# In the G stage of a product-key expert layer: the third product of a group moved behind the next compare, U's low parts taken out of the weight helper, expert selection finished four groups earlier

## The chip, the core and the metric

One core of a Trainium2 chip runs the whole program. The metric is the device time of one execution in microseconds (us), the median of several runs. TensorE (PE) multiplies matrices, VectorE (DVE) does elementwise work, ScalarE (ACT) does activations and copies, GpSimd (POOL) here mostly issues gathers, SyncE (SP) issues DMA transfers. Each engine works through its own list of instructions in a fixed order, and waits on semaphores where it needs a result of another.

## What is computed

The reference is one decoder layer on 512 tokens of 1024 features: a pooling mixer and latent attention, an output projection with layer norm, and then a product-key expert layer (PEER), which is where the change lies:

```python
q = (xc @ w_peer_q).reshape(TOK_CHUNK, PEER_HEADS, 2, PEER_HALF)
sc = jnp.einsum('thpd,hpnd->thpn', q, peer_keys)
s1, i1 = lax.top_k(sc[:, :, 0], PEER_TOPK)
s2, i2 = lax.top_k(sc[:, :, 1], PEER_TOPK)
...
s, j = lax.top_k(cand, PEER_TOPK)                 # 16 of 256 pairs, per head
idx = jnp.take_along_axis(cidx, j, axis=-1)       # 8 heads x 16 experts of 16384
gate = jax.nn.softmax(s, axis=-1)
a = jax.nn.gelu(jnp.einsum('thkd,td->thk', peer_u[idx], xc))
return jnp.einsum('thk,thkd->td', gate * a, peer_v[idx])
```

## The kernel before

Tokens lie in four tiles of 128. For the last tile (number 3) the kernel gathers the chosen rows of U and V. For tiles 0 to 2 it computes all 16384 experts densely: gelu(U h) for 128 blocks of 128 experts (a "U step" each), times a gate matrix G that is zero where an expert was not chosen, times V. Products that need float32 precision are made of three matmuls (`mm3`, L193: high by high, L196; high by low, L197; low by high, L198). High is the value rounded on ACT (`split`, L208), low is the rest, subtracted on DVE (`low`, L205).

The **G stage** builds the gate matrix and writes it to DRAM (`Gd`). `g_tiles` (L1061) runs over 3 tiles of 32 groups of four tokens. In iteration q it does, in program order:

- DVE: a compare of the iota row with the two expert indices of group q (`is_equal`, L1072, 1024 columns), which writes one-hot rows 0 and 1 of a buffer `o`; then for group q-1 the products of one-hot row 1 with two bf16 pieces of the gate (L1076, 1024 columns, into rows 2 and 3), and in place with the third piece (L1077, 512 columns). L1077 overwrites what L1076 reads.
- PE: twelve small bf16 matmuls of group q-4 (L1084), four tokens by three pieces. The first two of a token need L1076, the third needs L1077.
- ACT: the copy of group q-5 out of PSUM (L1089); every fourth one is followed by a DMA to `Gd` on SP (L1091).
- DVE: some instructions of the selection of the next tile, `top_second(t + 1)`: a generator whose yields are weights, advanced until their sum reaches `NTP * i` in group i of the tile. With i = 29 (`NQ - 1 - GP`) the rest of it is run, and `g_prep` (L1036) transposes its three results on PE (L1046), copies them on ACT (L1048, L1050) and cuts the gate into pieces on DVE (L1052, L1054).

`beside` (L1106) sets k-steps of U between these: 2.4 of them for an iteration, 8 to a U step, each one `mm3` of 384 columns. A U step (`u_parts`, L797) begins with the gelu of the step before (ACT, L818), then `weights`, which splits the block of the next step: its high part on ACT (L208) and, from here on, its low part on DVE (L205), at once. So ACT waits for PE to end a U step, L208 comes behind that, and L205 behind L208.

Ahead of the G stage the selection of tile 3 and that of tile 0 run side by side on DVE (`both`, L1118), with k-steps of U beside them. Behind it comes the **V stage**, which reads G back and multiplies by V. No planner orders anything: the program order of each engine is that in which the Python code emits it. Buffers come from a pool `F` of 17.

Of the kernel before, what the change touches and what calls it, by code (L numbers as in the profile page):

```python
# [10 lines left out]
F32R = mybir.dt.float32r  # L11
# [3 lines left out]
AF = mybir.ActivationFunctionType  # L15
# [5 lines left out]
P = 128  # L21
# [25 lines left out]
DT = 3  # L47
# [12 lines left out]
N_S2 = 33  # L60
SCF = 15
NPRE = 2
NTP = 0.36
GP = 2
NPRE2 = 8

# [83 lines left out]
def trace(ctx: ExitStack, tc: tile.TileContext, A, out):  # L150
# [28 lines left out]
    def wide(dt=F32, shape=(P, D)):  # L179
        return T("F", shape, dt)  # L180
# [12 lines left out]
    def mm3(o, pairs, first=True, last=True):  # L193
        n = len(pairs)
        for i, (lh, ll, rh, rl) in enumerate(pairs):
            pe.matmul(o, lh, rh, start=first and i == 0, stop=False)  # L196
            pe.matmul(o, lh, rl, start=False, stop=False)  # L197
            pe.matmul(o, ll, rh, start=False, stop=last and i == n - 1)  # L198
# [8 lines left out]
    def split(hi, lo, src, eng=None):  # L207
        act.activation(hi, src, AF.Copy)  # L208
        low(lo, src, hi, eng)


    jobs, live, ueng = [], {}, [pool]
    done = {"load": 0, "split": 0}

    def job(src, shape=(P, KD, P), eng=None, dst=None):
# [11 lines left out]
    def split_to(i):  # L227
        while done["split"] < min(i, len(jobs)):
            n = done["split"]
            load_to(n + 1)  # L230
            _, shape, eng, dst = jobs[n]
            w = live.pop(n)
            if dst is None:
                live[n] = wide(F32R, shape), wide(F32R, shape)
                split(*live[n], w, ueng[n % len(ueng)] if eng == "u" else eng)
            else:
                dst(w)
            done["split"] += 1

    def weights(i, ahead=3):  # L240
        split_to(i + 1)
        load_to(i + 1 + ahead)
        split_to(i + 2)
        return live.pop(i)
# [357 lines left out]
    for m in range(2):  # L602
        wh, wl = weights(juk[m])
        for h in range(3):
            p = bank()
# [191 lines left out]
    def u_parts():  # L797

        i = nu[0]
        if i >= NK or i - max(used[0], NBF) > N_BACK - 2:  # L800
            return
        nu[0] += 1
        while gelus:
            gelus.pop(0)()
        wh, wl = weights(ju[i])
        p = a_bank()[:, :ND]
        for k in range(KD):
            mm3(p, [(wh[:, k], wl[:, k], h2h[k][:, :ND], h2l[k][:, :ND])], first=k == 0, last=k == KD - 1)
            yield

        def gelu():
            if i >= NBF:
                back[i] = T("B", [P, ND])
            else:
                if i % 2 == 0:
                    bf[0] = wide()
                back[i] = bf[0][:, i % 2 * ND:(i % 2 + 1) * ND]
            act.activation(back[i], p, AF.Gelu)  # L818
        gelus.append(gelu)
# [241 lines left out]
    def g_tiles():  # L1061

        PB, L = TB // 4, LL
        oo, pp, parts, stg = {}, {}, {0: g_prep(0)}, None
        rows = lambda x, n: x.rearrange("p a j (i d) -> p (a j) i d", d=2) if n else x
        iota8 = iotab.rearrange("p (i d) -> p i d", d=2).unsqueeze(1).to_broadcast([P, 8, P // 2, 2])
        for q in range(DT * NQ + L + 1):
            t, i = divmod(q, NQ)
            if t < DT:

                o = oo[q] = wide(BF, (P, 4, 4, P))
                dve.tensor_tensor(rows(o[:, :2], 8), iota8, pairs(parts[t][0][:, i], 8), op=ALU.is_equal)  # L1072
            if 1 <= q <= DT * NQ:
                o, g = oo[q - 1], parts[(q - 1) // NQ][1][:, (q - 1) % NQ]
                one = o[:, 1:2].rearrange("p a j i -> p a (j i)").to_broadcast([P, 2, 4 * P])
                dve.tensor_mul(rows(o[:, 2:], 8), one, pairs(g[:, 1:], 8))  # L1076
                dve.tensor_mul(rows(o[:, 1:2], 4), rows(o[:, 1:2], 4), pairs(g[:, :1], 4))  # L1077
            if L <= q < DT * NQ + L:
                o = oo.pop(q - L)
                uid[0] += 1  # L1080
                p = pp[q - L] = psg.tile([P, 4, P], F32, name=f"gp_{uid[0]}", tag="gp", bufs=4)
                for j in range(4):
                    for n in (2, 3, 1):
                        pe.matmul(p[:, j], o[:, 0, j], o[:, n, j], start=n == 2, stop=n == 1)  # L1084
            if q > L:
                r = q - L - 1
                if r % PB == 0:
                    stg = T("G", [P, NK, TB])
                act.activation(stg[:, :, r % PB * 4:r % PB * 4 + 4], pp.pop(r).rearrange("p t i -> p i t"), AF.Copy)  # L1089
                if r % PB == PB - 1:  # L1090
                    sync.dma_start(Gd[:, r // PB], stg)  # L1091
            if t + 1 < DT:
                if i == 0:
                    nxt, spent = top_second(t + 1), 0.0
                while spent < NTP * i:
                    spent += next(nxt, 99.0)
                if i == NQ - 1 - GP:
                    for _ in nxt:
                        pass
                    parts[t + 1] = g_prep(t + 1)  # L1100
            yield KD * R_G[min(t, DT - 1)]

# [204 lines left out]
```

## Time and profile before

| | |
|---|---|
| runs | 1615.81, 1612.07, 1616.0 us; median 1615.81 |
| profiled execution | 1614.81 us, of which the traced span is 1613.1 us |
| mean granted TensorE clock | 0.975 |
| busy in the span | PE 1505.9 us (93%), DVE 1257.4 (78%), ACT 590.5 (37%), POOL 405.3 (25%) |
| G stage | 458.4 to 687.2 us of the span: tile 0 to 537.8, tile 1 to 623.4, tile 2 to the end |

A busy share is an average over stages with different limits, and PE's hides the G stage, where DVE is busier than PE. Times inside the span count from its start. In a timeline the first number is an instruction's start, the second its duration, and what stands in brackets is the idle time of its engine before it and what ended it. Instructions of one engine overlap a little: the distance between two starts is what one costs in a full queue, and it can be shorter than the duration.

### The profile page before, as it was taken

Reading aid. Unit: us, or ns where it says so; the run is one execution under the profiler, and the core shown is the slowest. Engines: PE = TensorE matmul, PEld = TensorE weight load, DVE = VectorE, ACT = ScalarE, POOL = GpSimd, SP = SyncE. Lnnn points to the kernel's source line nnn. Section 1 sums busy time; section 2 is a strip of 40 time slices with the busy share of each in tenths; the row PEclk is TensorE's granted clock in tenths of the full one; section 3 lists DMA queues with packets and bytes.
Section 4 is the critical chain, followed back from the end, with each engine's and each line's share of the span. In section 5 each row is a group of like instructions: output and inputs, shape, how many; then the busy total and the mean of one; then the engine's idle time right before and its main releaser. Section 6 shows DMA issues by size and latency. Waiting matters only on the chain.

```text
span 1613.1 us, 22579 instructions
## 1 busy us (share of the span) xinstructions
PE 1505.9 (93%) x8217; PEld 1294.1 (80%) x8217; DVE 1257.4 (78%) x2717; ACT 590.5 (37%) x909; POOL 405.3 (25%) x315
## 2 busy tenths in 40 slices
PE   5899999699888898969999999999999999999996
PEld 4665678578877777849999888898989888888984
DVE  5666556789999898947686877697788788778797
ACT  3353534223334443423342433343333333333342
POOL 0000101623100000013333343443333233333323
PEclk9999999899999998979999999999999999999998
DMA  8655103542234444689888899889889889888781
GB/s 327 216 183 201 67 26 124 188 128 76 99 106 171 144 180 147 220 265 329 303 318 301 306 320 323 303 315 334 314 286 343 288 315 335 303 317 318 277 302 74
DMA packets 147295, 382.70 MB, mean 237 GB/s; under 512 B 11312, under 2 KB 62544, under 8 KB 144112
## 3 DMA queue, kind: packets, MB, share of 16 engines
q1 hardware_dynamic: 109328, 243.56, 43.7%
q0 software_dynamic: 37856, 137.70, 24.0%
q8 instruction: 64, 1.05, 0.3%
q14 instruction: 47, 0.39, 0.1%
HBM read 351.86 MB, written 29.36 MB: 236 GB/s over the span
## 4 chain that ended last, share of the span: by engine, by line
PE 66%; DVE 23%; issue 3%; DMA 3%; ACT 2%; POOL 2%; SPq 0%; POOLq 0%; DVEq 0%; ACTq 0%
PE acc L197 10%; PE acc L198 10%; PE acc L196 9%; PE a L198 9%; PE a L196 9%; PE a L197 9%; DVE F L205 3%; DVE F L1076 3%; DVE F L1072 3%; PE ps L198 2%; PE ps L197 2%; PE ps L196 2%; DVE F L1077 2%; PE ps L662 1%; PE gp L1084 1%
## 5 line engine op out<-in xcount | busy, mean ns | idle before, releaser
L205 DVE TENSOR_TENSOR F<-F,F 128x1024 fp32r<-128x1024 f32 (+2 forms) x274 | 334.9, 1223 | 90.9 <-ACT F L208 63.6
L196 PE MATMUL a<-H,F 128*128 128x384 f32 (+1 forms) x1040 | 360.8, 347 | 3.9 <-ACT F L208 3.9
L198 PE MATMUL a<-H,F 128*128 128x384 f32 (+1 forms) x1040 | 353.9, 340 | 7.3 <-DVE F L205 5.2
L197 PE MATMUL a<-H,F 128*128 128x384 f32 (+1 forms) x1040 | 352.3, 339 | 0.0
L1137 POOL DMA_INDIRECT F<-in_u,cidx x128 | 159.2, 1243 | 553.3 <-PE acc L198 496.1
L196 PE MATMUL acc<-F,W 128*128 128x512 f32 x696 | 271.5, 390 | 15.3 <-ACT W L1203 15.3
L197 PE MATMUL acc<-F,W 128*128 128x512 f32 x696 | 273.1, 392 | 0.1
L198 PE MATMUL acc<-F,W 128*128 128x512 f32 x696 | 273.0, 392 | 0.0
L1137 POOL DMA_INDIRECT F<-in_v,cidx x128 | 147.9, 1155 | 273.4 <-DVE F L205 171.8
L198 PEld LDWEIGHTS a<-H,F 128*128 128x128 f32 x1040 | 197.4, 190 | 10.4 <-DVE F L205 6.9
L196 PEld LDWEIGHTS a<-H,F 128*128 128x128 f32 x1040 | 198.1, 190 | 8.3 <-ACT F L208 4.2
L197 PEld LDWEIGHTS a<-H,F 128*128 128x128 f32 x1040 | 197.9, 190 | 4.1
L1146 DVE SCALAR_TENSOR_TENSOR F<-F,F 128x1024 f32<-128x1024 f32 x128 | 153.3, 1220 | 59.4 <-DMA F<-in_u,cidx 59.3
L1159 DVE SCALAR_TENSOR_TENSOR Y<-F,a,Y 128x1024 f32<-128x1024 f32 x127 | 163.0, 1283 | 45.8 <-DMA F<-in_v,cidx 43.3
L208 ACT ACTIVATE F<-F 128x1024 fp32r<-128x1024 f32 (+2 forms) x164 | 169.6, 1036 | 54.4 <-DVE Y L1159 12.6
L1201 ACT ACTIVATE F<-F 128x1024 fp32r<-128x1024 f32 x128 | 134.9, 1054 | 144.3 <-DVE F L1146 72.0
L196 PEld LDWEIGHTS acc<-F,W 128*128 128x128 f32 x696 | 131.1, 188 | 40.8 <-ACT W L1203 15.5
L198 PEld LDWEIGHTS acc<-F,W 128*128 128x128 f32 x696 | 131.0, 188 | 27.6 <-DVE W L205 0.2
L197 PEld LDWEIGHTS acc<-F,W 128*128 128x128 f32 x696 | 131.0, 188 | 26.3 <-DVE F L205 0.6
L818 ACT ACTIVATE B<-a 128x384 f32<-128x384 f32 x122 | 59.3, 486 | 209.3 <-PE a L198 197.5
L1203 ACT ACTIVATE W<-B 128x384 fp32r<-128x384 f32 x110 | 57.8, 525 | 212.2 <-PE acc L197 114.0
L1084 PE MATMUL gp<-F 128*128 128x128 bf16 x1152 | 87.4, 221 | 13.3 <-DVE F L1076 6.0
(283 smaller groups left out, 1986.3 us busy)
## 6 DMA issues: line engine op xcount, KB each, us to landing
F<-in_ut SPq DMA_DIRECT2D x128, 512.0 KB
F<-in_v SPq DMA_DIRECT2D x128, 512.0 KB
F<-in_wada SPq DMA_DIRECT2D x48, 512.0 KB
Gd<-G SPq DMA_DIRECT2D x24, 1024.0 KB
G<-Gd SPq DMA_DIRECT2D x15, 1536.0 KB
F<-in_wpq SPq DMA_DIRECT2D x16, 512.0 KB
F<-in_wout SPq DMA_DIRECT2D x8, 512.0 KB
F<-in_win SPq DMA_DIRECT2D x8, 448.0 KB
```

What stands on the lines that cost most here:

```text
L196: pe.matmul(o, lh, rh, start=first and i == 0, stop=False)
L197: pe.matmul(o, lh, rl, start=False, stop=False)
L198: pe.matmul(o, ll, rh, start=False, stop=last and i == n - 1)
L205: dve.tensor_sub(lo, src, f(hi))
L208: act.activation(hi, src, AF.Copy)
L818: act.activation(back[i], p, AF.Gelu)
L1084: pe.matmul(p[:, j], o[:, 0, j], o[:, n, j], start=n == 2, stop=n == 1)
L1137: pool.indirect_dma_start(out=g, out_offset=None, in_=table, in_offset=bass.IndirectOffsetOnAxis(ap=cidx[:, k:k + 1], axis=0))
L1146: dve.scalar_tensor_tensor(g, g, 1.0, h2r[DT], op0=ALU.mult, op1=ALU.mult, accum_out=aT[:, k:k + 1])
L1159: dve.scalar_tensor_tensor(y3, g, aT[:, k:k + 1], y3, op0=ALU.mult, op1=ALU.add)
L1201: act.activation(Vhl[j][0], v, AF.Copy)
L1203: act.activation(W[j][0], w, AF.Copy)
```

## The change

Three edits. In `g_tiles` the product with two pieces now comes first in an iteration, then the compare of the next group, then the product in place. U's low parts, where they belong to DVE, are put on a list; the list is emptied behind the third k-step of the running U step, or at the start of the next. The selection is paced at 0.42 instead of 0.36, and its rest is run at i = 25, while `g_prep` stays at i = 29.

```diff
-NTP = 0.36
+NTP = 0.42
...
-    jobs, live, ueng = [], {}, [pool]
+    jobs, live, ueng, lows = [], {}, [pool], []
...
-                live[n] = wide(F32R, shape), wide(F32R, shape)
-                split(*live[n], w, ueng[n % len(ueng)] if eng == "u" else eng)
+                hi, lo = live[n] = wide(F32R, shape), wide(F32R, shape)
+                if eng == "u" and ueng[0] is dve:
+                    act.activation(hi, w, AF.Copy)
+                    lows.append((lo, w, hi))
+                else:
+                    split(hi, lo, w, ueng[n % len(ueng)] if eng == "u" else eng)
...
+    def low_now():
+        while lows:
+            low(*lows.pop(0))
+
     def weights(i, ahead=3):
+        low_now()
         split_to(i + 1)
...
             mm3(p, [(wh[:, k], wl[:, k], h2h[k][:, :ND], h2l[k][:, :ND])], first=k == 0, last=k == KD - 1)
+            if k == 2:
+                low_now()
             yield
...
             t, i = divmod(q, NQ)
+            if 1 <= q <= DT * NQ:
+                o1, g = oo[q - 1], parts[(q - 1) // NQ][1][:, (q - 1) % NQ]
+                one = o1[:, 1:2].rearrange("p a j i -> p a (j i)").to_broadcast([P, 2, 4 * P])
+                dve.tensor_mul(rows(o1[:, 2:], 8), one, pairs(g[:, 1:], 8))
             if t < DT:
 
                 o = oo[q] = wide(BF, (P, 4, 4, P))
                 dve.tensor_tensor(rows(o[:, :2], 8), iota8, pairs(parts[t][0][:, i], 8), op=ALU.is_equal)
             if 1 <= q <= DT * NQ:
-                o, g = oo[q - 1], parts[(q - 1) // NQ][1][:, (q - 1) % NQ]
-                one = o[:, 1:2].rearrange("p a j i -> p a (j i)").to_broadcast([P, 2, 4 * P])
-                dve.tensor_mul(rows(o[:, 2:], 8), one, pairs(g[:, 1:], 8))
-                dve.tensor_mul(rows(o[:, 1:2], 4), rows(o[:, 1:2], 4), pairs(g[:, :1], 4))
+                dve.tensor_mul(rows(o1[:, 1:2], 4), rows(o1[:, 1:2], 4), pairs(g[:, :1], 4))
...
-                if i == NQ - 1 - GP:
+                if i == NQ - 1 - GP - L:
                     for _ in nxt:
                         pass
+                if i == NQ - 1 - GP:
                     parts[t + 1] = g_prep(t + 1)
```

The order of PE, ACT, POOL and SP is what it was, instruction for instruction; only DVE's list is reordered, from 422 us of the span to the end of the G stage. In the changed program the lines have moved: the compare is L1087, the product with two pieces L1083, the product in place L1089, the selection's first line L961 (before: L950), its last L1038 (L1027), the gate's copies L1063 and L1065 (L1052 and L1054).

First place: DVE in tile 2, where no selection runs. The names F_989, F_996, F_998 are the one-hot buffers of three groups in a row, F_994 is a low part of U. Before:

```order
L205 TENSOR_TENSOR F_994_6151<-F_966_5952,F_993_6150 128x1024
L1072 TENSOR_TENSOR F_996_6161<-iotab_3649,sm2_955_5879 128x1024
L1076 TENSOR_TENSOR F_989_6128<-F_989_6128,gp3_957_5881 128x1024
L1077 TENSOR_TENSOR F_989_6128<-F_989_6128,gp3_957_5881 128x512
L1072 TENSOR_TENSOR F_998_6188<-iotab_3649,sm2_955_5879 128x1024
L1076 TENSOR_TENSOR F_996_6161<-F_996_6161,gp3_957_5881 128x1024
L1077 TENSOR_TENSOR F_996_6161<-F_996_6161,gp3_957_5881 128x512
```

And of the change, the same place:

```order
L1083 TENSOR_TENSOR F_989_6129<-F_989_6129,gp3_957_5880 128x1024
L1087 TENSOR_TENSOR F_996_6161<-iotab_3649,sm2_955_5878 128x1024
L1089 TENSOR_TENSOR F_989_6129<-F_989_6129,gp3_957_5880 128x512
L205 TENSOR_TENSOR F_994_6151<-F_966_5952,F_993_6150 128x1024
L1083 TENSOR_TENSOR F_996_6161<-F_996_6161,gp3_957_5880 128x1024
L1087 TENSOR_TENSOR F_998_6189<-iotab_3649,sm2_955_5878 128x1024
L1089 TENSOR_TENSOR F_996_6161<-F_996_6161,gp3_957_5880 128x512
```

Between the two products of one buffer there now stands the compare of the next, and the low part comes one group later.

Second place: DVE at the end of tile 0, where the selection of tile 1 ends. The names sm_811 and sm_812 (after: sm_797 and sm_798) are its results, sm_814 is the transposed gate. Before:

```order
L1072 TENSOR_TENSOR F_808_4868<-iotab_3649,sm2_685_4036 128x1024
L1076 TENSOR_TENSOR F_806_4842<-F_806_4842,gp3_687_4038 128x1024
L1077 TENSOR_TENSOR F_806_4842<-F_806_4842,gp3_687_4038 128x512
L1020 TENSOR_TENSOR F_756_4453<-F_756_4453,bt_728_4265 128x2x128
L1027 TENSOR_TENSOR sm_811_4888<-F_756_4453 128x128
L1027 TENSOR_TENSOR sm_812_4889<-F_756_4453 128x128
L1052 CAST gp3_815_4894<-sm_814_4893 128x32x8
```

And of the change:

```order
L1038 TENSOR_TENSOR sm_797_4778<-F_746_4395 128x128
L1038 TENSOR_TENSOR sm_798_4779<-F_746_4395 128x128
L1083 TENSOR_TENSOR F_794_4759<-F_794_4759,gp3_687_4038 128x1024
L1087 TENSOR_TENSOR F_799_4789<-iotab_3649,sm2_685_4036 128x1024
L1089 TENSOR_TENSOR F_794_4759<-F_794_4759,gp3_687_4038 128x512
L1083 TENSOR_TENSOR F_799_4789<-F_799_4789,gp3_687_4038 128x1024
L1087 TENSOR_TENSOR F_806_4824<-iotab_3649,sm2_685_4036 128x1024
L1089 TENSOR_TENSOR F_799_4789<-F_799_4789,gp3_687_4038 128x512
L205 TENSOR_TENSOR F_804_4817<-F_776_4628,F_803_4816 128x1024
L1083 TENSOR_TENSOR F_806_4824<-F_806_4824,gp3_687_4038 128x1024
L1087 TENSOR_TENSOR F_808_4849<-iotab_3649,sm2_685_4036 128x1024
```

The two results are made four groups ahead of the gate's first copy (L1063, five rows after the last one shown); before, they stood right in front of it.

Third place: DVE in the second group of tile 1, where the next selection begins. The name sm_833 is what ACT takes the exponential of, F_841 is a low part of U. Before:

```order
L950 TENSOR_TENSOR sm_833_5022<-F_455_2222 128x128
L954 CAST sm_834_5025<-F_455_2222 128x128
L956 TENSOR_SCALAR sm_835_5026<-sm_834_5025 128x128
L205 TENSOR_TENSOR F_841_5039<-F_800_4807,F_840_5038 128x1024
L1072 TENSOR_TENSOR F_843_5046<-iotab_3649,sm2_813_4892 128x1024
```

And of the change:

```order
L961 TENSOR_TENSOR sm_833_5022<-F_455_2222 128x128
L965 CAST sm_834_5025<-F_455_2222 128x128
L967 TENSOR_SCALAR sm_835_5026<-sm_834_5025 128x128
L1083 TENSOR_TENSOR F_830_5004<-F_830_5004,gp3_815_4894 128x1024
L1087 TENSOR_TENSOR F_843_5046<-iotab_3649,sm2_813_4892 128x1024
L1089 TENSOR_TENSOR F_830_5004<-F_830_5004,gp3_815_4894 128x512
L969 TENSOR_SCALAR sm_835_5026<-sm_835_5026 128x128
L971 TENSOR_SCALAR sm_837_5028<-sm_834_5025 128x128
L205 TENSOR_TENSOR F_841_5039<-F_802_4814,F_840_5038 128x1024
```

One whole group and two small instructions now stand between the selection's first three and the low part.

## Rows read from the trace of the kernel before

**Rows 1.** The page: busy time by engine, and shares of the chain that ended last.

```profile
PE 1505.9 (93%) x8217; PEld 1294.1 (80%) x8217; DVE 1257.4 (78%) x2717; ACT 590.5 (37%) x909; POOL 405.3 (25%) x315
...
PE 66%; DVE 23%; issue 3%; DMA 3%; ACT 2%; POOL 2%; SPq 0%; POOLq 0%; DVEq 0%; ACTq 0%
```

**Rows 2.** Windows, one for each tile: length, busy times, granted clock, DMA share, GB/s.

```profile
458.40:537.80 79.40, 66.97 (x571) 58.10 (x570) 76.04 (x153) 32.83 (x53) 0.00 (x0) 0.96 0.40 142
537.80:623.40 85.60, 72.93 (x633) 63.60 (x630) 77.08 (x154) 36.47 (x59) 0.00 (x0) 0.94 0.45 158
623.40:687.20 63.80, 61.74 (x616) 56.09 (x615) 62.41 (x107) 30.09 (x50) 0.00 (x0) 1.00 0.61 215
```

**Rows 3.** Groups by line, DVE, 458.4 to 687.2: busy, mean ns, idle before.

```profile
L1077 DVE TENSOR_TENSOR F<-F,gp 128x512 bf16<-128x512 bf16 x96 | 40.8, 425 | 3.3
L205 DVE TENSOR_TENSOR F<-F,F 128x1024 fp32r<-128x1024 f32 x28 | 34.3, 1225 | 9.0 <-ACT F L208 9.0
```

**Rows 4.** Timeline of DVE in tile 2: start, duration, instruction, idle before.

```profile
647.06 0.68 DVE L1072 TENSOR_TENSOR F<-iotab,sm 128x1024 bf16<-128x1024 bf16 x1
647.66 0.69 DVE L1076 TENSOR_TENSOR F<-F,gp 128x1024 bf16<-128x1024 bf16 x1
648.38 0.43 DVE L1077 TENSOR_TENSOR F<-F,gp 128x512 bf16<-128x512 bf16 x1
648.72 1.22 DVE L205 TENSOR_TENSOR F<-F,F 128x1024 fp32r<-128x1024 f32 x1
```

**Rows 5.** Timeline of DVE ahead of the G stage, two selections side by side.

```profile
443.04 1.28 DVE L1012 TENSOR_TENSOR F<-bt,sm 128x1024 bf16<-128x1024 bf16 x2
444.25 1.28 DVE L1014 TENSOR_TENSOR F<-F,sm 128x1024 bf16<-128x1024 bf16 x2
...
449.06 1.22 DVE L205 TENSOR_TENSOR F<-F,F 128x1024 fp32r<-128x1024 f32 x1
450.20 0.75 DVE L1018 TENSOR_TENSOR F<-F 128x512 bf16<-128x512 bf16 x2
```

**Rows 6.** Timeline of DVE, its idle times at the ends of tiles 0 and 1.

```profile
534.97 1.23 DVE L205 TENSOR_TENSOR F<-F,F 128x1024 fp32r<-128x1024 f32 x1 [1.83 <-ACT F L208]
...
541.11 0.28 DVE L950 TENSOR_TENSOR sm<-F 128x128 f32<-128x128 f32 x1
...
544.52 1.23 DVE L205 TENSOR_TENSOR F<-F,F 128x1024 fp32r<-128x1024 f32 x1 [2.73 <-ACT F L208]
...
622.26 1.23 DVE L205 TENSOR_TENSOR F<-F,F 128x1024 fp32r<-128x1024 f32 x1 [4.22 <-ACT F L208]
```

**Rows 7.** Timeline of PE at the transposes of tile 0's end.

```profile
530.02 0.69 PE L1046 MATMUL tr<-cst,sm 128*128 128x128 f32 x2 [6.90 <-DVE sm L1027]
```

**Rows 8.** Timeline of ACT at the start of tile 1.

```profile
541.43 0.31 ACT L952 ACTIVATE sm<-sm 128x128 f32<-128x128 f32 x1 [1.17 <-DVE sm L950]
```

**Rows 9.** Timeline of PE in tile 2: groups 59, 89, and 90 with 91.

```profile
619.32 0.84 PE L1084 MATMUL gp<-F 128*128 128x128 bf16 x12
...
679.18 0.84 PE L1084 MATMUL gp<-F 128*128 128x128 bf16 x12
...
680.45 1.51 PE L1084 MATMUL gp<-F 128*128 128x128 bf16 x24
```

**Rows 10.** Timeline of PE: three waits ahead of the G stage, one matmul more.

```profile
417.32 0.44 PE L198 MATMUL a<-H,F 128*128 128x384 f32 x1 [2.07 <-POOL F L203]
417.60 0.34 PE L196 MATMUL a<-H,F 128*128 128x384 f32 x1
...
425.33 0.69 PE L196 MATMUL a<-H,F 128*128 128x384 f32 x1 [3.90 <-ACT F L208]
...
450.33 0.69 PE L198 MATMUL a<-H,F 128*128 128x384 f32 x1 [4.92 <-DVE F L205]
```

**Rows 11.** Windows behind the wait of 3.90: columns as in rows 2.

```profile
425.30:430.60 5.30, 5.02 (x14) 4.51 (x15) 5.29 (x21) 1.30 (x2) 0.00 (x0) 0.50 0.36 148
```

**Rows 12.** Timeline of PE: the first matmul of the V stage.

```profile
703.23 0.80 PE L196 MATMUL acc<-F,W 128*128 128x512 f32 x1 [15.30 <-ACT W L1203]
```

## The prediction

> **What bounds the kernel now.** I read the page first: PE is busy 93% of the span and has 66% of the chain that ended last, DVE 23% [rows 1]. That is a mean over stages. The change touches one stage, so I asked for windows, one for each tile of the G stage [rows 2]. The reader is to compare DVE's busy time with the length: 76.0 of 79.4 us in tile 0, 77.1 of 85.6 in tile 1, 62.4 of 63.8 in tile 2, while PE has 67.0 and 72.9 in the first two. So the stage of 228.8 us is set by DVE, and DVE's time there is of two kinds.
>
> First what a group costs in DVE's full queue. Read the starts, not the durations [rows 4]: compare to first product 0.60 us, first product to product in place 0.72, from there to the next instruction 0.34; together 1.66. The compare of 0.68 is overtaken by 0.08, while the product in place starts only 0.03 after the end of the one whose input it overwrites. These 0.03 are the 3.3 us of idle time in front of 96 such products [rows 3]. A low part of U costs 1.14 from start to start (449.06 to 450.20 [rows 5]), and there are 28 [rows 3].
>
> Second its idle time: 9.0 us, all in front of U's low parts, all until ACT has the high part [rows 3]. Three of them make 8.8 [rows 6]. The first comes about so: PE has reached the transposes of the selection, which DVE has not yet finished, and stands for 6.90 us [rows 7]; what follows on PE, the end of a U step, is late, so its gelu on ACT is late, so the high part behind it, so DVE's low part: 1.83 us. The second, 2.73, is in part of another kind: ACT waits in its order for the selection's first instruction (541.11), takes the exponential at 541.43 [rows 8], and only then reaches the gelu and the high part.
>
> **The change, part by part.**
>
> *The product in place behind the next compare.* Nothing is added, nothing removed. The product in place now stands two behind the one that it has to wait for, with a compare between. I take 0.60 for each of the two large ones and 0.34 for the small one: 1.54 instead of 1.66, 0.12 a group. Is a wait on an instruction two places back free? The trace has such pairs: ahead of the G stage two selections run side by side, each L1014 needs the L1012 two places before it, and two of these 1024-column instructions take 444.25 - 443.04 = 1.21, that is 0.60 each [rows 5]. The first compare and its product now stand next to each other, and the last group has no compare behind it, so 94 groups gain: 94 x 0.12 = 11.3 us. The bounds are 0 (every instruction pays for its predecessor's end however they stand) and 11.3; I take the upper, as the pairs are the same kind of instruction.
>
> Here a rule of the Trainium skill speaks against it: VectorE: DVE Perf Modes, section "The DRAIN you can't avoid", says that the next operation does not start until the pipe of the one before is empty, and that chaining without semaphores does not avoid it. By that rule the new order would save nothing. The row disagrees for independent instructions (0.60 between starts, 0.68 of duration), and agrees only for the product in place; the measured starts decide.
>
> *The selection four groups earlier.* The transposes stand where they stood on PE, but their inputs are now made in group 25, and PE's matmuls ahead of them (group 25's) already need a product that DVE makes after that. So the waits of 6.90 go, and with them the lateness of gelu and high part: 1.83 and 4.22 of DVE's idle time, and the 0.2 left over. What is late next? In tile 1's second group ACT still waits for the selection's first instruction. From 541.11 to the low part's start the chain takes 3.41 us [rows 6], of which DVE could use 0.7 before. In the new order there stand the selection's three, one group (1.54) and two small ones between, some 2.4 us; about 1.0 of the 2.73 stays. The denser pacing costs a little: four more selection instructions stand directly behind the one that they wait for, at about 0.1 each: 0.4 us.
>
> *U's low parts later.* They move one group back in DVE's order. Within DVE the order of independent work costs nothing; the cover is that the high part is then surely there. Who waits for it? PE needs the low part at the third matmul of the next U step. PE runs up to three groups ahead of DVE's list; the low part used to be emitted 3.3 groups ahead of its use, now some 2.3, so PE will stand there up to one group (1.7 us) longer in tiles 0 and 1. PE has room: its 32 groups need 32 x 1.995 = 63.8 us at the rate of tile 2 (30 groups from 619.32 to 679.18 [rows 9]), and DVE will need some 74. So this wait replaces waits that PE had group by group. Ahead of the G stage it is not free: PE stands 4.92 us for a low part [rows 10], which now comes behind four half-size selection instructions more (2 x 0.67 from 450.20, taken twice [rows 5]): 1.34 later, less 0.6 which DVE gains there by filling earlier idle time. The G stage starts 0.7 later. Bounds: 0 to 1.4.
>
> *Tile 2, where PE becomes the slower one.* DVE would need 32 x 1.54 + 8 low parts x 1.14 = 58.4, 1.82 a group; PE needs 1.995 as long as U goes on. U ends at group 90 for want of buffers, and groups then take 0.7 [rows 9]. At the start of tile 2 PE stands near group 62: 28 x 1.995 + 1.3 + 5 x 0.7 + 0.7 = 61.4 us to the end of the last group, against 64.5 before (623.4 to 703.23 - 15.30 = 687.9 [rows 2, 12]). Gain 3.1, where DVE alone would give 4.
>
> *The sum.* Tiles 0 and 1: 62 x 0.12 = 7.4, and 8.8 - 1.0 = 7.8 of idle time, less 0.4: 14.8. Tile 2: 3.1. Start: -0.7. Together 17.2 us. Behind the last group everything is as before: the way through DRAM to the first V matmul, 15.30 us in which PE idles [rows 12], and a V stage whose lists are unchanged (in it a U step is emitted as a whole, so the deferred low part has nothing to pass on DVE). The profiled execution took 1614.8 us, span 1613.1 and 1.7 around it: 1614.8 - 17.2 = 1597.6. It lies 1.0 below the median of the runs shown and within them. I forecast 1597.5.
>
> **The rivals.**
>
> *A: the new order of the products saves nothing.* By the rule above. Then only the idle time goes, in tiles 0 and 1, and tile 2 stays DVE's: 7.8 + 0.2 - 0.4 - 0.7 = 6.9, 1608. For it: only that the product in place itself never was measured with something in between. Against it: the pairs [rows 5].
>
> *B: PE or buffers take part of it.* PE's list is 63.8 us a tile and a few transposes; if its waits for low parts don't fall into its free time, tiles 0 and 1 gain half: 1603 to 1606. For it: DVE's and PE's rates in tile 2 lie within a tenth. Against: ten us of room in each of the first two tiles.
>
> *C: slower.* One mechanism: PE's wait for the low part, at the start of each U step of tiles 0 and 1, becomes long enough for the clock to fall. After the waits of 3.90 and 4.92 it did: granted 0.50 (the 1.2 GHz level) for 5.3 us behind the first of them [rows 10, 11]; half of that, 2.6 us, is lost each time. A U step is 3.33 groups: 6.6 of PE work and 2.6 make 9.2, more than DVE's 7.7; 20 steps of it are 184 us for two tiles that took 165. With 3.1 back from tile 2 and 0.7 lost ahead: 1631. It decides if the waits come near those two in length. Against it: I expect under two, and after a wait of 2.07 PE went on at full speed, 0.34 for the next matmul [rows 10].
>
> *D: no change*, because the waits at the transposes turn up elsewhere, as waits of DVE for buffers that PE frees (each compare needs a buffer that PE read five groups before): 1612 to 1618. Against it: PE runs ahead.
>
> **How the numbers follow.** Forecast 0.72 (its own range 1594 to 1601), A 0.07, B 0.12, C 0.04, D 0.05. Differences under 0.3%, 4.8 us, can't be told from none. Forecast, A and B lie beyond it: faster 0.91; D: same 0.05; C: slower 0.04. The range is 1592 to 1607: it takes in B and most of A, and below leaves 2 us for the runs' own spread and for a late start of the G stage that doesn't happen.
>
> **What would show it.** The G stage should last about 212 us instead of 228.8. In its timeline the compare, the product in place and the first product should start 0.60, 0.34 and 0.60 apart, with no idle time in front of the product in place. DVE's idle time until ACT's high parts should be 1 to 2 us instead of 9.0. PE should have no wait for L1038 at the transposes, the granted clock should be 1.00 in tiles 0 and 1, and new waits of PE for DVE's low parts should appear, each under two us. It would be wrong if DVE is under 95% busy in tiles 0 and 1, if PE has waits of over three us there, or if the V stage changes its length.

## The result, and the profile after

The changed kernel takes 1594.41 us (median of four runs, 1592.38 to 1597.79); the kernel before 1615.9 beside it. The ratio is 0.987, 95% interval 0.9847 to 0.9893. The forecast was 1597.5, with a range of 1592 to 1607. A second timing, below, gave 0.9872.

The line numbers have moved: the compare L1072 is now L1087, the product of two pieces L1076 is L1083, the product in place L1077 is L1089, the gate matmuls L1084 are L1096, U's high part L208 is L236 (L205 stays), and the transposes L1046 are L1057.

From the page of the kernel after: busy times, and shares of the chain that ended last [rows 1]. Next to nothing moves here, although 17.2 us of span are gone: the shares are means over 1600 us.

```profile
PE 1504.0 (94%) x8217; PEld 1294.2 (81%) x8217; DVE 1248.0 (78%) x2717; ACT 591.4 (37%) x909; POOL 408.7 (26%) x315
...
PE 67%; DVE 23%; DMA 4%; issue 2%; ACT 2%; POOL 2%; SPq 0%; DVEq 0%; POOLq 0%; ACTq 0%
```

Windows of the kernel after, one for each tile, with the columns of [rows 2]:

```profile
461.00:535.70 74.70, 67.83 (x603) 60.43 (x602) 74.15 (x153) 34.69 (x55) 0.00 (x0) 0.98 0.46 165
535.70:610.50 74.80, 66.62 (x615) 58.49 (x613) 73.37 (x153) 34.30 (x58) 0.00 (x0) 1.00 0.48 174
610.50:670.60 60.10, 59.93 (x603) 55.08 (x602) 60.01 (x107) 30.05 (x50) 0.00 (x0) 1.00 0.59 210
```

Behind the length stand the busy times of PE, of PEld (TensorE's weight loads) and of DVE. DVE now fills 74.15 of 74.70, 73.37 of 74.80 and 60.01 of 60.10 us: the stage is DVE's list and next to nothing else. The granted clock, 0.96 and 0.94 in the first two tiles before, is 0.98 and 1.00.

Groups by line, DVE, over the G stage after (busy, mean ns, idle before), to be read against [rows 3]:

```profile
L1089 DVE TENSOR_TENSOR F<-F,gp 128x512 bf16<-128x512 bf16 x96 | 39.7, 413 | 0.0
L205 DVE TENSOR_TENSOR F<-F,F 128x1024 fp32r<-128x1024 f32 x28 | 34.3, 1223 | 0.9 <-ACT F L236 0.9
```

Both idle times went: 3.3 to 0.0 in front of the product in place, 9.0 to 0.9 in front of the low parts. Timeline of DVE after, in tile 1 and tile 2 (start, duration, instruction, idle before), against [rows 4, 6]:

```profile
541.64 1.23 DVE L205 TENSOR_TENSOR F<-F,F 128x1024 fp32r<-128x1024 f32 x1 [0.92 <-ACT F L236]
...
647.53 0.68 DVE L1083 TENSOR_TENSOR F<-F,gp 128x1024 bf16<-128x1024 bf16 x1
648.13 0.67 DVE L1087 TENSOR_TENSOR F<-iotab,sm 128x1024 bf16<-128x1024 bf16 x1
648.73 0.41 DVE L1089 TENSOR_TENSOR F<-F,gp 128x512 bf16<-128x512 bf16 x1
649.07 1.21 DVE L205 TENSOR_TENSOR F<-F,F 128x1024 fp32r<-128x1024 f32 x1
```

The starts lie 0.60, 0.60 and 0.34 apart, where before it was 0.60, 0.72 and 0.34. PE's waits in the stage after (line, releaser: us in total, times, longest us):

```profile
PE a L198 <- DVE F L205: 12.6, 12, 2.3
PE gp L1096 <- DVE F L1089: 1.9, 6, 0.5
PE tr L1057 <- ACT sm L1059: 0.5, 2, 0.3
```

The waits of 6.9 us at the transposes [rows 7] are gone; in their place PE waits twelve times for a low part, the longest 2.3. Timeline of PE after: the wait ahead of the stage, the longest waits for a low part in tile 0 and in tile 1, and the first matmul of the V stage, against [rows 10, 12]:

```profile
453.08 0.69 PE L198 MATMUL a<-H,F 128*128 128x384 f32 x1 [5.23 <-DVE F L205]
...
489.91 0.44 PE L198 MATMUL a<-H,F 128*128 128x384 f32 x1 [2.34 <-DVE F L205]
490.19 0.84 PE L1096 MATMUL gp<-F 128*128 128x128 bf16 x12
...
493.48 1.44 PE L1096 MATMUL gp<-F 128*128 128x128 bf16 x12
...
560.27 0.45 PE L198 MATMUL a<-H,F 128*128 128x384 f32 x1 [2.23 <-DVE F L205]
560.56 0.84 PE L1096 MATMUL gp<-F 128*128 128x128 bf16 x12
...
685.54 0.80 PE L196 MATMUL acc<-F,W 128*128 128x512 f32 x1 [14.23 <-ACT W L1216]
```

Behind the wait of 2.23 PE goes on at full speed (0.84 for twelve gate matmuls, as in [rows 9]); behind the one of 5.23 a matmul takes 0.69. Behind the wait of 2.34 twelve gate matmuls take 0.84 at first and 1.44 three microseconds later, and a window of the kernel after shows why, with the columns of [rows 2]:

```profile
491.30:494.70 3.40, 3.40 (x20) 3.09 (x19) 3.40 (x8) 0.36 (x1) 0.00 (x0) 0.50 0.02 5
```

The granted clock is 0.50 here, the 1.2 GHz level; this one stretch makes the 0.98 of tile 0. DVE is busy all through it (3.40 of 3.40 us), so it costs the stage no idle time of DVE.

### The profile page after: what moved, and what is told of

The parts are those of the page before. It is cut to its first block, busy times and chain, and to the rows that moved or that the text cites. A ratio compares the mean times of both kernels' runs of the same rounds, so it can differ in the third digit from the quotient of the medians.

```text
span 1595.9 us, 22580 instructions
## 1 busy us (share of the span) xinstructions
PE 1504.0 (94%) x8217; PEld 1294.2 (81%) x8217; DVE 1248.0 (78%) x2717; ACT 591.4 (37%) x909; POOL 408.7 (26%) x315
## 4 chain that ended last, share of the span: by engine, by line
PE 67%; DVE 23%; DMA 4%; issue 2%; ACT 2%; POOL 2%; SPq 0%; DVEq 0%; POOLq 0%; ACTq 0%
PE acc L197 10%; PE acc L198 10%; PE acc L196 10%; PE a L198 9%; PE a L196 9%; PE a L197 9%; DVE F L1083 3%; DVE F L205 3%; DVE F L1087 3%; PE ps L198 2%; PE ps L197 2%; PE ps L196 2%; DVE F L1089 2%; DMA F<-in_v 1%; PE ps L671 1%
## 5 line engine op out<-in xcount | busy, mean ns | idle before, releaser
L205 DVE TENSOR_TENSOR F<-F,F 128x1024 fp32r<-128x1024 f32 (+2 forms) x274 | 334.4, 1221 | 89.6 <-ACT F L236 31.7
L1214 ACT ACTIVATE F<-F 128x1024 fp32r<-128x1024 f32 x128 | 134.9, 1054 | 146.1 <-DMA F<-in_v 67.1
L236 ACT ACTIVATE F<-F 128x1024 fp32r<-128x1024 f32 x120 | 126.5, 1054 | 30.5 <-DVE Y L1172 14.2
L198 PE MATMUL ps<-H,F 128*128 128x512 f32 x176 | 74.3, 422 | 11.5 <-POOL F L203 6.2
```

The costliest lines, as they stand in the source:

```text
L205: dve.tensor_sub(lo, src, f(hi))
L236: act.activation(hi, w, AF.Copy)
L1214: act.activation(Vhl[j][0], v, AF.Copy)
```

## The experiments

All tables here come from the traces of single executions. A tile lasts from its first compare to the next tile's, the stage from the first compare to the end of the last gate matmul; "idle" is DVE's idle time inside the stage, counting gaps above 0.06 us. "Ratio" is the measured time over that of the kernel before. Three theories were put to the test. M is the prediction's: DVE's list sets the stage, so the new order of the products and the idle time in front of the low parts are two gains that add up. R is the rule that the new order saves nothing. P says that PE's two waits of 6.9 us at the transposes, with the lower clock behind them, are the time, so that the earlier selection alone brings nearly all of it.

| kernel | ratio, 95% | tile 0 | tile 1 | tile 2 | stage | idle |
|---|---|---|---|---|---|---|
| before | | 79.39 | 85.63 | 64.52 | 229.54 | 8.97 |
| products alone | 0.9958 [0.9944, 0.9972] | 76.38 | 82.22 | 62.60 | 221.21 | 12.06 |
| low parts alone | 0.9970 [0.9958, 0.9982] | 77.86 | 80.10 | 65.97 | 223.93 | 3.09 |
| selection alone | 0.9962 [0.9949, 0.9975] | 77.87 | 81.77 | 64.25 | 223.89 | 2.73 |
| products, selection | 0.9898 [0.9883, 0.9912] | 74.64 | 77.77 | 60.08 | 212.49 | 3.05 |
| products, low parts | 0.9898 [0.9884, 0.9912] | 74.76 | 76.32 | 64.78 | 215.85 | 6.46 |
| low parts, selection | 0.9960 [0.9944, 0.9976] | 77.82 | 78.61 | 65.34 | 221.77 | 0.80 |
| all three | 0.9870 [0.9847, 0.9893] | 74.72 | 74.77 | 60.79 | 210.28 | 0.92 |
| low parts later still | 0.9927 [0.9914, 0.9941] | 79.72 | 76.22 | 63.35 | 219.29 | 7.94 |
| every other low part on POOL | 0.9985 [0.9977, 0.9994] | 81.28 | 78.78 | 66.65 | 226.71 | 9.41 |

**The new order of the products alone.** The kernel before with this edit and no other:

```diff
+            if 1 <= q <= DT * NQ:
+                ...
+                dve.tensor_mul(rows(o1[:, 2:], 8), one, pairs(g[:, 1:], 8))
             if t < DT:
                 ...
             if 1 <= q <= DT * NQ:
-                ...
-                dve.tensor_mul(rows(o[:, 2:], 8), one, pairs(g[:, 1:], 8))
-                dve.tensor_mul(rows(o[:, 1:2], 4), rows(o[:, 1:2], 4), pairs(g[:, :1], 4))
+                dve.tensor_mul(rows(o1[:, 1:2], 4), rows(o1[:, 1:2], 4), pairs(g[:, :1], 4))
```

> The kernel before with the first edit alone: product in place behind the next compare. Theory M (DVE sets tiles 0 and 1, PE's backlog sets tile 2): 94 groups x 0.12 us leave DVE's list, of which the backlog that PE has after the transposes of tile 1 takes a little back: 9 to 11 us faster, 1605 to 1607 where before is 1616. The idle time of DVE in front of U's low parts stays at 8 to 10 us. Rival R (an instruction pays for its predecessor's end however they stand): 0, and the first product and the compare start 0.68 or more apart. Rival P (PE is the bound, its waits are what counts): under 3 us.

It took 1608.95 us against 1615.0. R and P fall, but M was too high, and with another reason: the stage lost 8.3 us, not the full 94 x 0.12 = 11.3, and what takes the rest back is not PE's backlog but idle time of DVE, which M had expected to stay at 8 to 10 us and which is 12.06. The idle time in front of the low parts tells why; timeline of DVE in this kernel:

```profile
532.77 1.23 DVE L205 TENSOR_TENSOR F<-F,F 128x1024 fp32r<-128x1024 f32 x1 [2.08 <-ACT F L208]
...
541.94 1.23 DVE L205 TENSOR_TENSOR F<-F,F 128x1024 fp32r<-128x1024 f32 x1 [2.73 <-ACT F L208]
...
616.53 1.23 DVE L205 TENSOR_TENSOR F<-F,F 128x1024 fp32r<-128x1024 f32 x1 [4.76 <-ACT F L208]
622.93 1.23 DVE L205 TENSOR_TENSOR F<-F,F 128x1024 fp32r<-128x1024 f32 x1 [0.56 <-ACT F L208]
```

Before it was 1.83, 2.73 and 4.22 [rows 6], and 0.19 behind them. DVE reaches the low part sooner, ACT's high part is no sooner there, and in tile 2 five waits of 0.41 to 0.56 appear that were not there. Idle time grows by 3.1; 11.3 - 3.1 = 8.2.

**The low parts alone.**

```diff
-                split(*live[n], w, ueng[n % len(ueng)] if eng == "u" else eng)
+                if eng == "u" and ueng[0] is dve:
+                    act.activation(hi, w, AF.Copy)
+                    lows.append((lo, w, hi))
...
+            if k == 2:
+                low_now()
```

> The kernel before with the second edit alone: U's low parts one group later. M: the low part gives the high part 1.7 us more, so of DVE's waits of 1.83 and 2.73 some 3.4 us go; the 4.22 at the end of tile 1 count for nothing, because PE has a backlog there; 0.3 to 0.7 is lost at the start of the G stage: 2 to 4 us faster, 1612 to 1614. PE waits 13.8 us at the transposes as before. P: 0, or slower by the new waits of PE for low parts (some 12 us in all in the changed kernel): 1616 to 1628.

1611.33 against 1615.0, just beyond the expected 1612 to 1614. The stage is 5.6 shorter, which is more than was expected, and the idle time 5.9: the low part behind the third k-step alone takes most of the waits for ACT away, the 4.22 at the end of tile 1 among them, which M had counted for nothing. Of the 3.09 that are left 1.2 are waits for ACT, the rest are waits of compares for buffers that PE frees. Tile 2 grows by 1.4. In this trace the V stage is 2.3 us longer than before, so its span shows only 2.6 of the 5.6.

**The selection alone.**

```diff
-NTP = 0.36
+NTP = 0.42
...
-                if i == NQ - 1 - GP:
+                if i == NQ - 1 - GP - L:
                     for _ in nxt:
                         pass
+                if i == NQ - 1 - GP:
                     parts[t + 1] = g_prep(t + 1)
```

> The kernel before with the third edit alone: selection done four groups ahead of the transposes. M: PE's 13.8 us of waiting go, but only the DVE idle time that they cause counts, 1.83 + 4.22, less 0.4 for the denser pacing: 5 to 6 us faster, 1610 to 1611; the wait of 2.73 behind the exponential stays. P: all of PE's 13.8 us and its slow clock behind them come back: 14 us or more faster, 1602 or less.

1609.58 against 1615.0, as M said; P's 14 us fall. PE's waits at the transposes are gone here (none above 0.3), but only 5.7 of the stage go with them. One idle time of DVE is left in the trace of this kernel, and it is the second of [rows 6], at its old size:

```profile
545.26 1.23 DVE L205 TENSOR_TENSOR F<-F,F 128x1024 fp32r<-128x1024 f32 x1 [2.73 <-ACT F L208]
```

**Products and selection, the low parts as before.** The changed kernel with

```diff
-                if eng == "u" and ueng[0] is dve:
-                    act.activation(hi, w, AF.Copy)
-                    lows.append((lo, w, hi))
...
+                split(*live[n], w, ueng[n % len(ueng)] if eng == "u" else eng)
...
-            if k == 2:
-                low_now()
```

> The change without its second edit: low parts where they were. M: 11 + 5.5, with 2 to 3 us of idle time left in front of the low part behind the exponential: 15 to 18 us faster, 1598 to 1601, that is 2 to 4 us short of the whole change. P: as the whole change or better, since PE has no new waits for low parts: 1594 or less.

1598.46 against 1615.0: as M said. The 2.73 us at tile 1's start stay, and that is the difference of 2.2 us to the whole change: the low parts' move is worth about two microseconds once the other two edits are in, against 5.6 by itself. This reading rests on the traces; the intervals of the two ratios overlap.

**The whole change again,** beside the next three, with no edit:

> The whole change once more, for a closer interval beside the partial ones: 1593 to 1597, 18 to 22 us below the kernel before. G stage 210 to 211 us; one idle time of DVE over 0.1 us in it, 0.9 in front of the low part behind the exponential.

1595.57 against 1615.09, ratio 0.9872 [0.9856, 0.9888]; its stage lasts 210.29 us.

**Products and low parts, the selection as before.** The changed kernel with

```diff
-NTP = 0.42
+NTP = 0.36
...
-                if i == NQ - 1 - GP - L:
+                if i == NQ - 1 - GP:
```

> The change without its third edit: the selection ends right in front of its transposes. M: PE still waits 13 us at the transposes, so its backlog sets tile 2: product order and low parts together give 10 to 12 us, 1603 to 1605, a little less than the sum of the two alone (8.3 + 5.6 of the G stage), since both want the same free time of PE. Rival A (edits add up freely): 14 us.

1598.81 against 1615.09, a gain of 16.3 by the medians; the traced execution took 1601.0, and its span is 14 us shorter than before. By the medians that is more than either expectation. In the stage it is what rival A of this expectation said: 13.7, where the two edits alone give 8.3 + 5.6 = 13.9. They add up, and M's reason, that PE's backlog takes a part, falls. PE still waits 5.93 and 5.39 us at the transposes, yet of the three idle times of [rows 6] 0.38, 1.56 and 0.95 are left, with 1.07 for a buffer of PE's and some of half a microsecond in tile 2: 6.46 in all. 11.3 + (8.97 - 6.46) = 13.8; the stage lost 13.7.

**Low parts and selection, the products as before.** This is rival A as a kernel:

```diff
-            if 1 <= q <= DT * NQ:
-                ...
-                dve.tensor_mul(rows(o1[:, 2:], 8), one, pairs(g[:, 1:], 8))
...
-                dve.tensor_mul(rows(o1[:, 1:2], 4), rows(o1[:, 1:2], 4), pairs(g[:, :1], 4))
+                ...
+                dve.tensor_mul(rows(o[:, 2:], 8), one, pairs(g[:, 1:], 8))
+                dve.tensor_mul(rows(o[:, 1:2], 4), rows(o[:, 1:2], 4), pairs(g[:, :1], 4))
```

> The change without its first edit. This is rival A of the prediction as a kernel: 7 to 9 us faster, 1606 to 1608, with 1 us of idle time left. If the order of the products saves nothing, the whole change and this one come out alike.

1608.55 against 1615.09. DVE's idle time is as small as in the whole change (0.80), and yet the stage takes 221.77: the 11.5 us to 210.28 are the order of the products and nothing else, since that is the only difference of the two kernels.

**The low parts behind the eighth k-step.** Rival C's condition, made on purpose. The changed kernel with

```diff
-            if k == 2:
+            if k == 7:
                 low_now()
```

> The whole change with the low parts emitted behind the eighth k-step of a U step instead of the third, 5 k-steps or 2.1 groups later. M: PE now stands 3 to 4 us at the third matmul of most U steps of tiles 0 and 1, as long as the waits that were followed by half the clock; a U step then takes PE longer than DVE's 7.7 us: rival C of the prediction made on purpose, 5 to 25 us slower than the whole change, with granted clocks below 0.95 in tiles 0 and 1. If late low parts don't matter as long as DVE is full: within 2 us of the whole change.

1604.16, 8.6 us more than the whole change beside it. PE now waits 18.0 us for low parts in ten waits, where the whole change has 12.6 in twelve; three of the ten, not most, are over three us. Timeline of PE in this kernel, behind its longest wait:

```profile
467.87 0.69 PE L198 MATMUL a<-H,F 128*128 128x384 f32 x1 [4.90 <-DVE F L205]
468.36 1.50 PE L1096 MATMUL gp<-F 128*128 128x128 bf16 x12
469.62 0.67 PE L196 MATMUL a<-H,F 128*128 128x384 f32 x1
```

Twelve gate matmuls take 1.50 us, where behind a wait of 2.23 they take 0.84. Windows over most of tiles 0 and 1 of this kernel, columns as in [rows 2]:

```profile
467.00:540.00 73.00, 66.19 (x559) 59.49 (x560) 67.08 (x135) 28.17 (x48) 0.00 (x0) 0.89 0.42 152
540.00:610.00 70.00, 62.88 (x561) 56.61 (x560) 68.51 (x142) 32.61 (x54) 0.00 (x0) 0.95 0.48 177
```

The clock falls to 0.89 and 0.95, and DVE is busy in 92% of the first window. DVE's idle time is 7.0 us longer than in the whole change, 6.1 of it in front of compares, nearly all until PE has freed a buffer. So rival C's mechanism exists: PE is late enough here for DVE to wait for it. How much of that is the clock and how much the longer waits themselves, this kernel does not separate. With the third k-step one stretch at the lower level is left in the stage (491.3 to 494.7 above), and DVE does not wait for PE behind it.

**Every other low part of the stage on POOL.** DVE's list is now the bound, so less of it should be faster. The changed kernel with

```diff
-                if eng == "u" and ueng[0] is dve:
+                if eng == "u" and ueng[n % len(ueng)] is dve:
...
+    ueng[:] = [dve, pool]
     beside(g_tiles(), 0)
+    ueng[:] = [dve]
```

A low part that belongs to POOL (L203) is not put on the list: it is emitted at once behind its high part (L208).

> The whole change, with every other low part of U of the G stage made on POOL instead of DVE. Theory M (DVE's queue sets the first two tiles, 74.8 us with DVE 74.2 and 73.4 busy): 14 low parts x 1.14 = 16 us leave DVE, about 5 a tile; DVE's work of tiles 0 and 1 falls to 69-70 us, still over PE's 66-68, so each tile comes to 69-70 and the G stage from 210 to 200-202; the kernel at 1585-1588. A low part on POOL took 2.34 us in a row of before, so its end comes 1.2 us later: PE's waits for low parts are one or two us longer each where they stand now (12 of them, 12.6 us in all), which may give back 2-4 of this. Rival: DVE and POOL hold each other up while both run (products of 0.41 and compares of 0.60 become longer): no gain, 1594, or slower, 1600.

1612.88 against 1614.45: nearly the whole gain is lost. The rival of that expectation holds in its mechanism, and the loss is larger than it said (1594 to 1600). Groups by line in this kernel, first DVE's, then POOL's:

```profile
L1087 DVE TENSOR_TENSOR F<-iotab,sm 128x1024 bf16<-128x1024 bf16 x95 | 71.0, 747 | 9.2 <-POOL F L203 6.7 <-PE gp L1096 1.5 <-PE a L197 1.0
L1083 DVE TENSOR_TENSOR F<-F,gp 128x1024 bf16<-128x1024 bf16 x96 | 68.2, 710 | 0.0
L1089 DVE TENSOR_TENSOR F<-F,gp 128x512 bf16<-128x512 bf16 x96 | 46.6, 485 | 0.0
...
L203 POOL TENSOR_TENSOR F<-F,F 128x1024 fp32r<-128x1024 f32 x14 | 72.0, 5142 | 182.2 <-ACT F L208 139.6 <-DVE F L205 24.1 <-DVE F L1083 18.6
```

POOL's low parts take 5.14 us on average, with 2.40 the shortest, and DVE's products in place, 413 ns in the whole change, 485. Fourteen low parts at 1.135 from start to start took 15.9 us of work off DVE, yet the stage is 16.4 us longer than in the whole change and DVE's idle time only 8.5: the instructions left on DVE became some 24 us longer together, an estimate from these numbers (16.4 - 8.5 + 15.9). Two places of the timelines of POOL and DVE show what happens (the first two rows are POOL's):

```profile
506.62 11.89 POOL L203 TENSOR_TENSOR F<-F,F 128x1024 fp32r<-128x1024 f32 x1 [12.87 <-ACT F L208]
529.09 2.63 POOL L203 TENSOR_TENSOR F<-F,F 128x1024 fp32r<-128x1024 f32 x1 [10.58 <-ACT F L208]
...
515.63 0.68 DVE L1083 TENSOR_TENSOR F<-F,gp 128x1024 bf16<-128x1024 bf16 x1
518.54 0.69 DVE L1087 TENSOR_TENSOR F<-iotab,sm 128x1024 bf16<-128x1024 bf16 x1 [2.23 <-POOL F L203]
...
529.40 2.61 DVE L1089 TENSOR_TENSOR F<-F,gp 128x512 bf16<-128x512 bf16 x1
531.93 0.68 DVE L1083 TENSOR_TENSOR F<-F,gp 128x1024 bf16<-128x1024 bf16 x1
```

At 529.40 DVE stands until POOL is done: 2.61 us for an instruction of 0.41. At 506.62 POOL stands: DVE's instructions keep their full pace until 516.3, POOL ends 2.2 us after DVE has run out of buffers, and by then DVE waits for POOL, and PE for the low part (5.16 us at 518.56). The two do not share; one works and the other stands. Which of them stands, the runs do not settle.

**The low parts ahead of the stage on POOL.** PE waits there 5.23 us for one of them. In the changed kernel the line that gives the low parts to DVE is moved from ahead of the two selections to behind them:

```diff
-    ueng[:] = [dve]
...
+    ueng[:] = [dve]
```

> The whole change, with the low parts of U ahead of the G stage made on POOL instead of DVE, those of the G stage as they were. Theory M: 6 low parts x 1.2 = 7.3 us leave DVE between 425 and 461 us, and PE's wait of 5.23 us for the low part at 453 mostly goes; the G stage begins 2-5 us earlier and the kernel ends at 1590-1592. Rival (POOL takes 2.34 us for a low part and is itself busy there, so that PE waits for POOL in its place): the G stage begins at the same point within 1 us, 1593-1596.

1592.86 us, 0.9868 [0.9848, 0.9888], not to be told from the whole change. The stage starts 37.24 us after the selections' first instruction, against 37.07: what the rival forecast, though not by its reason, a wait of PE for POOL (there is one, of 1.8 us). Timeline of DVE and PE in this kernel:

```profile
442.71 3.49 DVE L1025 TENSOR_TENSOR F<-F,sm 128x1024 bf16<-128x1024 bf16 x2
...
449.54 1.28 DVE L1025 TENSOR_TENSOR F<-F,sm 128x1024 bf16<-128x1024 bf16 x2
...
458.12 0.69 PE L1057 MATMUL tr<-cst,sm 128*128 128x128 f32 x2 [4.63 <-DVE sm L1038]
```

A pair of products that takes 1.28 takes 3.49 while POOL makes a low part, so that DVE is no sooner done, and PE's wait moves from the low part to the transposes.

**Both moves to POOL.**

> The whole change with both: the low parts ahead of the G stage on POOL and every other one of the G stage on POOL. Theory M: the two gains add, 1581-1586. Rival of both: no gain, 1593 or slower.

1613.49, ratio 0.9994 [0.9981, 1.0007]: again the rival; its stage takes 224.59 us. No version is clearly faster than the changed kernel.

## Why the prediction was right

*DVE sets the stage.* Shown in three ways. One sum fits the table: the stage loses 11.3 us where the products are in the new order, and besides the amount by which DVE's idle time falls, less 0.4 where the selection is denser. For the six partial kernels that gives 8.2, 5.9, 5.8, 16.8, 13.8 and 7.8 us, measured are 8.3, 5.6, 5.7, 17.1, 13.7 and 7.8; for the whole 19.0, measured 19.3. PE enters this sum only through the idle time. Second, in every kernel of the table but one the last gate matmul ends 0.77 us after DVE's last product. The one is that with the low parts behind the eighth k-step (1.69 us): there PE has a part of its own, and the sum gives 11.9 where 10.3 are measured. And the two kernels with half of the stage's low parts on POOL show the other sign: what lengthens DVE's instructions and its idle time lengthens the stage.

*The new order of the products.* 0.60, 0.60, 0.34, as forecast from the pairs of [rows 5]; 11.5 us by the kernel that lacks only this. The section of the Trainium skill from which rival A was made (VectorE: DVE Perf Modes, "The DRAIN you can't avoid") adds to its rule that a next instruction that is not held starts earlier. The rows agree with that limit, and rival A took the rule without it: independent instructions of 0.68 us start 0.60 apart, and behind one independent instruction the product in place starts with no loss.

*The selection four groups earlier.* No wait for it at the transposes, DVE's idle time at the ends of tiles 0 and 1 gone, as forecast. Of the 2.73 at tile 1's start 0.92 are left, where about 1.0 was worked out; that part needs the low parts' move, for with the selection alone the 2.73 stay.

*The low parts.* The forecast was that they cost nothing in the stage but a wait of PE of up to one group, under two us: two are longer (2.34 and 2.23), the next is 1.82. The forecast clock of 1.00 was nearly met: behind the 2.34 it is 0.50 for 3.4 us, so tile 0 has 0.98. DVE did not wait for that. What the prediction did not say is that this edit also takes idle time away by itself, 5.9 us of the same 9.0 that the selection takes; so it is a second cure for one ill, worth 2.2 with the other in place. Ahead of the stage, the low part at 449.06 [rows 5] now starts at 451.81 in a program part that began 2.4 us later in this execution; the stage begins 0.27 later in relation to that, where 0.7 was forecast.

*Tile 2* was the step that failed in its reason. The forecast was that PE becomes the slower one there, 61.4 us; it took 60.8, with DVE busy in 60.01 of 60.10 us. PE did fall behind DVE, by 4.7 us at group 89, but once U had ended it caught up and waited for DVE again at the end (timeline of PE after):

```profile
666.58 3.85 PE L1096 MATMUL gp<-F 128*128 128x128 bf16 x62
670.60 0.72 PE L1096 MATMUL gp<-F 128*128 128x128 bf16 x10 [0.17 <-DVE F L1089]
```

So DVE sets this tile too, with nine low parts in it, not eight: 32 x 1.54 + 9 x 1.135 = 59.5.

*The sum.* The forecast was 17.2 us, and the span lost 17.2 (1613.1 to 1595.9), but not by the same parts, so that the totals meet this closely is luck: the stage gave 19.3 instead of 17.9 (tiles 0 and 1 15.5 for 14.8, tile 2 3.7 for 3.1), the way to the V stage 1.1 instead of 0, the V stage took 0.6 more, the start cost 0.3 instead of 0.7, and the 2.4 us by which the selections began later lie ahead of everything that was changed, in a stretch that is the same in both kernels. The traced execution is also the slowest of the four; by the medians the gain is 21.5 us here and 19.5 in the second timing, whose trace has the same stage (210.29) and selections that begin 0.6 later. The 0.6 of the V stage are no sign of a change in it: over the eleven other traces it lasts 908 to 912 us, where the two here have 909.8 and 910.4.

*The rivals.* A would have left the stage some 11 us longer (the kernel without the new order is 11.5 longer), B 6 to 9; D is excluded by the result itself. C did not come, but its condition was put wrongly. The prediction tied it to waits near 3.90 and 4.92, with the wait of 2.07 that was followed by full speed against it; in the kernel after the clock fell behind 2.34, and with the low parts behind the eighth k-step behind 2.15 and, as the last section shows, behind 1.74. What kept C away from the changed kernel is that PE's waits there are few and short enough for DVE never to wait for PE.

## What to carry to other kernels

Read the starts of an engine's instructions, not their durations: where an instruction starts only after its predecessor's end while others overlap, put something independent between. Before a low gain is put down to one edit, sum the idle time of the engine that bounds the stage: two edits that remove the same idle time don't add (5.6 and 5.7 us of the stage alone, 7.8 together), and an edit that makes the bounding engine faster turns a part of its gain into waiting unless what it waits for comes sooner too. Giving two-operand work of a full DVE to POOL was no relief here: it cost 16.4 us of a stage of 210.

## What the runs showed of the hardware

POOL and DVE hold each other up completely: a subtraction on POOL took 2.40 us at its shortest and 12.89 at its longest beside bf16 products of DVE, and a product of 0.41 us took 2.61 beside POOL. The Trainium skill, SBUF — State Buffer, section "Who interferes with whom", says that a DVE instruction with two SBUF inputs contends with a GpSimd instruction that reads SBUF, and calls the ports that they share an exclusive lock; the rows agree. They add that POOL can stand through nineteen DVE instructions that follow each other without a gap (506.39 to 516.31), and that it ends only 2.2 us behind the last of them, nearly the 2.40 us of its shortest.

TensorE's clock: the length of the wait before it does not tell by itself whether it falls. Behind waits of 2.07 [rows 10] and 2.23 us PE went on at the full rate. Behind waits of 4.90, 4.92 and 5.23 matmuls ran at the lower of the two levels, but so they did behind 2.34 (above), and behind these two, the first of the kernel after, ahead of its stage, the second of the kernel with the low parts behind the eighth k-step; each with a window of its kernel:

```profile
419.71 0.69 PE L198 MATMUL a<-H,F 128*128 128x384 f32 x1 [2.04 <-POOL F L203]
419.70:423.00 3.30, 3.29 (x10) 3.29 (x11) 3.30 (x35) 0.00 (x0) 0.00 (x0) 0.50 0.03 5
...
591.94 0.45 PE L198 MATMUL a<-H,F 128*128 128x384 f32 x1 [1.74 <-DVE F L205]
592.60:596.00 3.40, 3.40 (x18) 3.25 (x15) 3.37 (x8) 0.60 (x1) 0.00 (x0) 0.50 0.02 5
```

What else decides it, no run here was made to show.
